# Low-rank weights and small constants prepared behind the first half's transposed input, and three low parts of the second half's input made by ScalarE and GpSimd

## The chip, the cores and the metric

The kernel runs on one core of one Trainium2 chip. The metric is the device time of one execution in microseconds; several runs are taken and their median is given. The engines are TensorE (PE: matmul, with PEld for its weight loads), VectorE (DVE), ScalarE (ACT), GpSimd (POOL) and SyncE (SP), which issues nearly all DMAs.

## The reference

One layer of a hybrid decoder trunk over a sequence of 1024 tokens with 1024 channels, in float32: a token mixer and a gated feed-forward part, each between two RMS norms.

```python
h = _rms_norm(x, norm_pre_mix)
# mixer: one projection p = h @ w_in; two groups of its columns
u, q = p[..., :1024], p[..., 1024:]
q = q + (_token_shift(q) - q) * mu            # r, k, v and the low-rank inputs wd, ad, gd
wf = decay_w0 + tanh(wd) @ decay_up           # decay of the recurrence
a  = sigmoid(iclr_a0 + ad @ iclr_up)
g  = sigmoid(gd) @ gate_up
y  = _wkv7(r, decay, k, v, -kk, kk * a)       # recurrence over the tokens, 8 heads of 64
rwkv_out = (_head_group_norm(y) + bonus) * g
c = silu(_layer_norm(_causal_dwconv(u[..., :512] * sigmoid(u[..., 512:]), cconv_w, 31 taps)))
x = x + _rms_norm(concat([rwkv_out, c]) @ w_out, norm_post_mix)
# feed-forward: ffn_up, a causal convolution of 3 taps, gelu(gate) * up, ffn_down
x = x + _rms_norm(_conv_ffn(_rms_norm(x, norm_pre_ffn)), norm_post_ffn)
```

## The kernel before

A float32 matmul is made of three faster ones: each operand is split into a high part (rounded to the matmul's type, float32r) and a low part (what the rounding left), and high times high, high times low and low times high are summed in one PSUM bank. A weight tile arrives as `wr`; ScalarE casts it to `wh` (L168), GpSimd subtracts to get `wl` (L168). The input of the projections is split in the same way, into the pairs `h`.

The 1024 tokens are worked in two halves of 512. For a half, `load_rows` (L307) loads four blocks of 128 token rows, `norm_rows` (L324 to L328) scales each row by its inverse norm, and `channels` (L280 to L295) transposes the rows by TensorE (L155) into PSUM banks and takes from each bank two readings: ScalarE writes the high part with the norm's gain as scale (L293), VectorE the low part (L295). A bank is free for TensorE again only when both have read it. There are two banks each with the tags `pe` and `pb`; `channels` takes them in the turn `pe`, `pb`, `pb`. In the first half a bank holds two channel tiles of 256 tokens, in the second half one tile of 512 tokens.

The first half's projections (`project`, into a `pb` bank) come right behind its transposes. The second half's transposes stand in the middle of the first half's work: VectorE then runs the 31 taps of the causal convolution (L432), each adding to one accumulator in the bank `pc`, and the first projections of the second half follow.

At the start `setup_mixer` also loads the two low-rank weights (`decay_up` and `iclr_up`, stacked in `lora`), casts them on ScalarE into `lw` (L254), subtracts their low rows on GpSimd (L256), and prepares small constants from the parameter table on VectorE (L260 to L269): one minus mu, halves of some biases, and halved convolution taps.

The order on each engine is made when the kernel is built: a scheduler takes the instructions by the priority of the stream in which they were written (`PRIO`; lower numbers come first, and parts under `high_priority` before others), with its own idea of how long each takes. `issue_after` holds the instructions written under it behind a given one. A change in one place can therefore also move instructions far behind it. One such stretch is the end of the mixer: there the last recurrence chunks, the convolution's layer norm (`conv_norm`: transposes `pc<-const,co`, norm, transposes `pc<-const,t`, then L453 on ScalarE, which writes `co`), the first nine feed-forward columns (`ffn_pair`: matmuls `pb<-f`, evacuation L911, a gelu L931), and the output projection (matmuls `pb<-wm,l`, its input split by L168 into `l<-mixr` and `l<-co`) share the engines. Each change between the functions of L453 and L931 costs ScalarE a table load.

DMAs are issued by SP in one queue; a new one waits until the one eight places before it has landed. The parameter table `params` holds the norm's gain, which L293 and L295 read.

Of the kernel before, what the change touches and what calls it, by code (L numbers as in the profile page):

```python
# [13 lines left out]
F32 = mybir.dt.float32  # L14
F32R = mybir.dt.float32r
BF16 = mybir.dt.bfloat16
AF = mybir.ActivationFunctionType
ALU = mybir.AluOpType
# [4 lines left out]
P = 128  # L23
# [3 lines left out]
HALF = 512  # L27
# [4 lines left out]
D_RWKV = 512  # L32
# [4 lines left out]
CONV_W = 31  # L37
# [32 lines left out]
POFF = {}  # L70
# [30 lines left out]
class Trunk:  # L101
# [130 lines left out]
    def setup_mixer(self, ctx):  # L232
        nc, tc, a = self.nc, self.tc, self.a
        pool = lambda name, bufs=1: ctx.enter_context(tc.tile_pool(name=name, bufs=bufs))
        cp = pool("mconst")
        self.mix = pool("mix")
        self.banks = {"pb": 2, "pc": 1, "pe": 2}
        self.xs = [self.psum.tile([P, 512], F32, name=f"xs{g}") for g in range(2)]
        self.wa = cp.tile([P, HALF], F32, name="wa")

        self.dw = cp.tile([P, 16 + 1024], F32, name="dw")
        nc.gpsimd.memset(self.dw[0:64, 528:1040], 0.0)
        self.Y = self.psum.tile([P, 512], F32, name="Y")


        self.lora = cp.tile([G_LORA, D_RWKV], F32, name="lora")
        nc.sync.dma_start(self.lora, a["lora"][:G_LORA, 2])
        self.lw = cp.tile([96, 2, D_RWKV], F32R, name="lw")  # L250
        for e in range(2):
            raw = self.wtile("wr", [P, D_RWKV])
            nc.sync.dma_start(raw, a["lora"][:, e])
            nc.scalar.copy(self.lw[:, e], raw[0:96])  # L254
            low = self.lw[64:96, e]
            nc.gpsimd.tensor_tensor(low, raw[64:96], low.bitcast(F32), ALU.subtract)  # L256
        self.lx = cp.tile([96, 2, QUARTER], F32R, name="lx")
        n = POFF["k_k"]
        self.omu = cp.tile([P, n], F32, name="omu")
        nc.vector.tensor_scalar(self.omu, self.params[:, :n], -1.0, 1.0, ALU.mult, ALU.add)  # L260

        self.hw0 = cp.tile([P, 8], F32, name="hw0")
        nc.vector.tensor_scalar(self.hw0, self.params[:, POFF["w0"]:POFF["w0"] + 8], 0.5, None, ALU.mult)
        self.ka = cp.tile([P, 8], F32, name="ka")
        ka = self.params[:, POFF["k_a"]:POFF["k_a"] + 4]
        nc.vector.tensor_scalar(self.ka[:, 0:4], ka, 0.5, None, ALU.mult)
        nc.vector.tensor_scalar(self.ka[:, 4:8], ka, -0.5, 1.0, ALU.mult, ALU.add)
        cw = self.params[:, POFF["cw"]:POFF["cw"] + 4 * CONV_W]
        nc.vector.tensor_scalar(cw, cw, 0.5, None, ALU.mult)  # L269
        self.carry = cp.tile([P, n], F32, name="carry")  # L270
        self.ccarry = cp.tile([P, 4, 32], F32, name="ccarry")[:, :, :CONV_W - 1]


    def channels(self, rows, gname, hs, toks, tags=("pn",), diags=None):


        nc = self.nc
        n = len(rows) * P
        per = 512 // n
        for b, k0 in enumerate(range(0, KT, per)):  # L280
            ps = self.bank(tags[b % len(tags)])
            for i in range(per):
                k = k0 + i
                for t, row in enumerate(rows):
                    o = (k % 4) * P
                    out, src = ps[:, i * n + t * P:i * n + (t + 1) * P], row[k // 4][:, o:o + P]
                    if diags is None:
                        self.transpose(out, src)
                    else:
                        self.mm(out, src, diags[t])  # L290
            parts = [(self.par(gname, k0 + i), ps[:, i * n:(i + 1) * n], *hs[k0 + i]) for i in range(per)]
            for g, pv, hi, lo in parts:
                self.mark_hi = nc.scalar.activation(hi[:, toks], pv, AF.Copy, scale=g)  # L293
            for g, pv, hi, lo in parts:
                self.mark_lo = nc.vector.scalar_tensor_tensor(lo[:, toks], pv, g, hi[:, toks].bitcast(F32), ALU.mult, ALU.subtract)  # L295

# [563 lines left out]
    def norm_ffn(self, h, row, piece, hs, ahead=2, tags=("pn",), dg=None, pool=None):  # L860
# [16 lines left out]
        for t in range(4):  # L877
            if t == ahead:
                channels(0)
            tt = 4 * h + t  # L880
            rs = slice(tt * P, (tt + 1) * P)
            x, s = row(), sf[:, t]
            nc.sync.dma_start(x, self.a["x"][rs])
            for c in range(2):
                m = piece()
                nc.sync.dma_start(m, self.mixd[rs, cut(c)])
                nc.vector.scalar_tensor_tensor(x[:, cut(c)], m, r[:, 4 + t:5 + t], x[:, cut(c)], ALU.mult, ALU.add)
                nc.scalar.activation(m, x[:, cut(c)], AF.Square, accum_out=s[:, c:c + 1])
            nc.sync.dma_start(self.x1d[rs], x)
            nc.vector.tensor_tensor(s[:, 2:3], s[:, 0:1], s[:, 1:2], ALU.add)  # L890
            self.rstd(s[:, 3:4], s[:, 2:3], 1.0 / D, RMS_EPS)
            if dg is None:
                nc.scalar.activation(x, x, AF.Copy, scale=s[:, 3:4])
            else:
                nc.vector.tensor_scalar(dg[:, t], self.con("ident"), s[:, 3:4], None, ALU.mult)
                diags.append(dg[:, t])
            rows.append((x[:, :512], x[:, 512:]))
            yield
        if ahead == 4:
            channels(0)  # L900
            yield
        channels(1)

    def taps(self, h, i, br, ps, acc):
# [371 lines left out]
    def mixer(self, sts):  # L1276
        nc, tc = self.nc, self.tc
# [78 lines left out]

        def channels(rows, hs):
            with self.stream("norm"):
                self.channels(rows, "pre_mix", hs, slice(0, HALF), ("pe", "pb", "pb"))

        cut = lambda t: (t[:, :512], t[:, 512:])
        with self.stream("norm"):
            two = [self.tl("l8", [P, 2, D]) for _ in range(2)]
            rows = [cut(two[t // 2][:, t % 2]) for t in range(4)]
            with self.stream("first"):
                self.load_rows(0, rows)
            hs = self.pairs("h")
            for b in range(2):
                two = rows[2 * b:2 * b + 2]
                self.norm_rows(two)  # L1370
                self.channels(two, "pre_mix", hs, slice(b * QUARTER, (b + 1) * QUARTER), ("pe", "pb", "pb"))
        self.R = self.tl("r", [P, NH, CH])
        nc.vector.memset(self.R[64:128], 0.0)
        project(0, hs, "k0 w k1 r0 r1")
        with self.stream("norm"):
            two = self.tl("mixr", [P, 2, D])
            rows = [cut(two[:, t]) for t in range(2)]
# [10 lines left out]
        project(0, hs, "u2 u3")  # L1388
        hs = self.pairs("h")
        channels(rows, hs)  # L1390
        mixes[0] = self.tl("mixr", [P, 4, HALF])
        prepare(1)
# [106 lines left out]
```

## Time and profile before

| | us |
|---|---|
| median of 3 runs | 1254.76 (1251.8 to 1254.91) |
| the profiled execution | 1252.95 |
| its span in the profile | 1251.2 |
| mean granted TensorE clock | 0.987 |
| busy: VectorE, ScalarE, GpSimd | 900.3, 729.4, 507.3 |

The profile gives for each engine what it ran and when, in us from the start of the span. A row of the timeline reads: start, duration, engine, line, operation, output<-input, how many were merged into the row, and, in brackets, how long the engine had been idle before it and what ended that. A row of the stage windows reads: the stretch and its length, then the busy time of TensorE, its weight loads, VectorE, ScalarE and GpSimd, each with its number of instructions, then the granted TensorE clock (1.00 is full), the DMA engines' busy share and GB/s.

### The profile page before, as it was taken

What the parts mean: (1) busy time and instruction counts of PE and PEld (TensorE: products, weight loads), DVE (VectorE), ACT (ScalarE), POOL (GpSimd) and SP (SyncE); (2) the same over time, 40 slices, a digit from 0 to 9 for tenths busy, and PEclk for the clock granted to TensorE, in tenths of its full rate; (3) what the DMA queues carried; (4) which work ended last, traced back from release to release, by engine and by line L of the source; (5) the groups of instructions that cost most, each with busy time, mean ns of one, the idle gap of its engine ahead of it and who ended that gap; (6) DMA issues with size and microseconds to landing.
All of it is one profiled execution on the core that took longest, in us unless ns stands there. A gap on an engine that the chain in (4) does not pass through costs nothing.

```text
span 1251.2 us, 22983 instructions
## 1 busy us (share of the span) xinstructions
PE 1204.7 (96%) x8424; PEld 985.3 (79%) x8424; DVE 900.3 (72%) x1558; ACT 729.4 (58%) x1515; POOL 507.3 (41%) x447
## 2 busy tenths in 40 slices
PE   5989998999999989999999999999999999999997
PEld 4767776787778977878889888888888888888886
DVE  5285998898669999998630655666656679479668
ACT  6563564565954676566752577876555566545452
POOL 4343330001103331354463499998888850000002
PEclk8999998999999999999999999999999999999999
DMA  7645442333343362222364798894222335337413
GB/s 244 177 122 141 134 135 64 97 123 125 110 125 93 99 200 96 77 86 77 110 181 120 287 314 299 294 310 151 85 75 77 101 128 169 99 109 223 133 59 134
DMA packets 102912, 180.97 MB, mean 145 GB/s; under 512 B 14896, under 2 KB 21424, under 8 KB 102800
## 3 DMA queue, kind: packets, MB, share of 16 engines
q1 hardware_dynamic: 102800, 179.51, 46.0%
q8 instruction: 66, 1.08, 0.4%
q14 instruction: 46, 0.38, 0.1%
HBM read 138.44 MB, written 41.03 MB: 143 GB/s over the span
## 4 chain that ended last, share of the span: by engine, by line
PE 62%; DVE 6%; DMA 1%; ACT 1%; issue 1%; POOL 0%; POOLq 0%; DVEq 0%; ACTq 0%
PE pb L140 27%; PE xs L140 16%; PE pe L140 14%; PE Y L140 2%; PE pc L140 2%; DVE pc L432 2%; DMA pt<-mixd 1%; PE pc L155 1%; DMA mixd<-t 0%; PE pe L155 0%; DVE m L168 0%; DVE sub L607 0%; DVE x L1123 0%; DVE dw L609 0%; DVE t L798 0%
## 5 line engine op out<-in xcount | busy, mean ns | idle before, releaser
L168 POOL TENSOR_TENSOR wl<-wr,wh 128x512 fp32r<-128x512 f32 (+1 forms) x175 | 230.0, 1316 | 218.2 <-ACT wh L168 183.9
L140 PE MATMUL pb<-h,wh 128*128 128x512 f32 (+3 forms) x720 | 229.0, 397 | 3.1 <-ACT wh L168 1.6
L140 PE MATMUL pb<-f,wh 128*128 128x512 f32 x648 | 203.7, 395 | 2.1 <-ACT wh L168 1.7
L168 ACT CAST wh<-wr 128x512 fp32r<-128x512 f32 (+1 forms) x214 | 131.4, 615 | 126.1 <-issue 37.3
L432 DVE SCALAR_TENSOR_TENSOR pc<-c,params,pc 128x512 f32<-128x512 f32 x232 | 174.3, 751 | 8.1 <-ACT pc L429 4.1
L140 PEld LDWEIGHTS pb<-h,wh 128*128 128x128 f32 (+2 forms) x720 | 131.5, 188 | 35.8 <-ACT wh L168 3.7
L140 PE MATMUL pb<-h,wl 128*128 128x512 f32 (+3 forms) x360 | 146.2, 406 | 2.2 <-POOL wl L168 2.0
L140 PEld LDWEIGHTS pb<-f,wh 128*128 128x128 f32 x648 | 121.1, 189 | 27.9 <-ACT wh L168 2.1
L140 PE MATMUL pb<-f,wl 128*128 128x512 f32 x324 | 128.7, 398 | 0.9 <-POOL wl L168 0.9
L162 POOL TENSOR_TENSOR ss<-var,mhalf 128x1 f32<-128x1 f32 x16 | 12.9, 810 | 221.0 <-DVE var L161 220.2
L1077 POOL TENSOR_TENSOR b<-b,b 128x512 f32<-128x512 f32 x72 | 93.2, 1297 | 2.1 <-DMA b<-ffn_down 0.7
L140 PEld LDWEIGHTS pb<-h,wl 128*128 128x128 f32 (+2 forms) x360 | 67.4, 187 | 20.7 <-POOL wl L168 4.6
L140 PE MATMUL xs<-f,wh 128*128 128x512 f32 x240 | 74.2, 390 | 0.4 <-DVE act L974 0.4
L168 POOL TENSOR_TENSOR wl<-b,wh 128x512 fp32r<-128x512 f32 x48 | 65.8, 1372 | 19.3 <-ACT wh L168 19.3
L140 PEld LDWEIGHTS pb<-f,wl 128*128 128x128 f32 x324 | 61.2, 189 | 14.8 <-POOL wl L168 2.2
L168 ACT CAST wh<-b 128x512 fp32r<-128x512 f32 x48 | 29.7, 618 | 59.9 <-PE pb L140 20.5
L140 PE MATMUL pe<-f,wh 128*128 128x512 f32 x208 | 64.1, 389 | 0.0
L722 POOL TENSOR_TENSOR XG<-r,GE 64x256 f32<-64x256 f32 x30 | 19.9, 666 | 87.5 <-DVE r L741 82.8
L140 PEld LDWEIGHTS xs<-f,wh 128*128 128x128 f32 x240 | 44.9, 188 | 10.1 <-DVE act L974 0.8
L193 ACT CAST wh<-wr 128x512 fp32r<-128x512 f32 (+2 forms) x44 | 26.5, 604 | 43.5 <-PE pb L140 31.1
L168 ACT CAST a<-act 128x512 fp32r<-128x512 f32 x50 | 30.0, 619 | 33.4 <-PE Y L140 18.9
L168 ACT CAST w<-wr 128x512 fp32r<-128x512 f32 x38 | 23.5, 622 | 40.9 <-PE Y L140 20.0
(421 smaller groups left out, 2948.8 us busy)
## 6 DMA issues: line engine op xcount, KB each, us to landing
wr<-ffn_up SPq DMA_DIRECT2D x99, 256.0 KB, 3.3
wr<-w_in SPq DMA_DIRECT2D x80, 256.0 KB, 2.9
b<-ffn_up SPq DMA_DIRECT2D x52, 256.0 KB, 2.7
b<-ffn_down SPq DMA_DIRECT2D x44, 256.0 KB, 4.6
sums<-b SPq DMA_DIRECT2D x44, 256.0 KB, 4.2
wr<-sums SPq DMA_DIRECT2D x44, 256.0 KB, 2.7
lows<-wl SPq DMA_DIRECT2D x40, 256.0 KB, 3.3
wl<-lows SPq DMA_DIRECT2D x40, 256.0 KB, 2.7
```

What stands on the lines that cost most here:

```text
L140: return self.nc.tensor.matmul(out, lhsT, rhs, start=start, stop=stop, skip_group_check=skip)
L155: self.nc.tensor.transpose(out, in_, self.con("ident")[:n, :n])
L162: self.nc.gpsimd.tensor_tensor(out, v[:, :n], self.mhalf[:, :n], ALU.pow)
L168: return self.nc.scalar.copy(hi, src), eng.tensor_tensor(lo, src, hi.bitcast(F32), ALU.subtract)
L193: self.nc.scalar.copy(hi, raw)
L432: nc.vector.scalar_tensor_tensor(out, c[:, j:j + HALF], w(j), acc, ALU.mult, ALU.add)
L722: nc.gpsimd.tensor_tensor(x[64:128], R[64:128, gs], w.GE[64:128, c, gs].unsqueeze(2).broadcast_to([64, 4, CH]), ALU.mult)
L1077: sub = lambda o, x, y, op=ALU.subtract: self.nc.gpsimd.tensor_tensor(o, x, y, op)
```

## The change

Three things change in the code. The low-rank weights and the small constants move from `setup_mixer` into a function of their own, `setup_later`, which is called behind the first half's transposed input: the weights are held behind its last high part, the constants behind its last low part. The low-rank weights are loaded into buffers with the tag `t2` instead of weight buffers. And in the second half, for the channel tiles 1, 3 and 5, VectorE no longer makes the low part: ScalarE copies the scaled tile in full precision into an SBUF buffer `pt`, and GpSimd subtracts the high part from it.

```diff
 def setup_mixer(self, ctx):
     self.lw = cp.tile([96, 2, D_RWKV], F32R, name="lw")
-    for e in range(2):
-        raw = self.wtile("wr", [P, D_RWKV])
-        nc.sync.dma_start(raw, a["lora"][:, e])
-        nc.scalar.copy(self.lw[:, e], raw[0:96])
-        low = self.lw[64:96, e]
-        nc.gpsimd.tensor_tensor(low, raw[64:96], low.bitcast(F32), ALU.subtract)
...
-    nc.vector.tensor_scalar(self.omu, self.params[:, :n], -1.0, 1.0, ALU.mult, ALU.add)
...
+def setup_later(self):
+    nc = self.nc
+    with self.tc.issue_after(self.mark_hi.ins):
+        for e in range(2):
+            raw = self.tl("t2", [P, D_RWKV])
+            nc.sync.dma_start(raw, self.a["lora"][:, e])
+            nc.scalar.copy(self.lw[:, e], raw[0:96])
+            low = self.lw[64:96, e]
+            nc.gpsimd.tensor_tensor(low, raw[64:96], low.bitcast(F32), ALU.subtract)
+    with self.tc.issue_after(self.mark_lo.ins):
+        nc.vector.tensor_scalar(self.omu, self.params[:, :POFF["k_k"]], -1.0, 1.0, ALU.mult, ALU.add)
...
 def channels(self, rows, gname, hs, toks, tags=("pn",), diags=None, pooled=()):
...
+    if k0 in pooled:
+        for g, pv, hi, lo in parts:
+            whole = self.tl("pt", [P, HALF])
+            nc.scalar.activation(whole, pv, AF.Copy, scale=g)
+            nc.gpsimd.tensor_tensor(lo[:, toks], whole, hi[:, toks].bitcast(F32), ALU.subtract)
+        continue
...
-    self.channels(rows, "pre_mix", hs, slice(0, HALF), ("pe", "pb", "pb"))
+    self.channels(rows, "pre_mix", hs, slice(0, HALF), ("pe", "pb", "pb"), pooled=(1, 3, 5))
...
         self.channels(two, "pre_mix", hs, slice(b * QUARTER, (b + 1) * QUARTER), ("pe", "pb", "pb"))
+    self.setup_later()
```

Line numbers of the changed kernel are about 10 higher behind the first edit (L293 is then L297, L453 is L463). The order of the instructions moves at three places.

First, SP's queue at the start of the program, from the last rows of the first half's input on (`l`, then `params`, `lora`, the weights `wr`, and `mixr`, the second half's rows). Before:

```order
L307 DMA l_4_129<-x 128x512 x4
L218 DMA params<-params 128x370
L219 DMA const<-consts 128x449
L249 DMA lora<-lora 96x512
L253 DMA wr_109<-lora 128x512
L253 DMA wr_113<-lora 128x512
L185 DMA wr_274<-w_in 128x512
```

And with the change:

```order
L317 DMA l_2_116<-x 128x512 x4
L185 DMA wr_274<-w_in 128x512
L185 DMA wr_281<-w_in 128x512
L185 DMA wr_340<-w_in 128x512
L218 DMA params<-params 128x370
L219 DMA const<-consts 128x449
L249 DMA lora<-lora 96x512
L265 DMA t_41_257<-lora 128x512
```

Three loads of projection weights now stand ahead of the parameters; on ScalarE two weight casts stand ahead of the first high part, and the low-rank casts behind the last one.

Second, VectorE at the second half's transposed input (`h`: low parts, `pc`: convolution taps). Before:

```order
L295 SCALAR_TENSOR_TENSOR h_1938<-pe_1953,params,h_1937 128x512
L432 SCALAR_TENSOR_TENSOR pc_1737<-c_1659,params,pc_1737 128x512
L295 SCALAR_TENSOR_TENSOR h_1940<-pb_1960,params,h_1939 128x512
L295 SCALAR_TENSOR_TENSOR h_1942<-pb_1967,params,h_1941 128x512
L432 SCALAR_TENSOR_TENSOR pc_1737<-c_1659,params,pc_1737 128x512
L295 SCALAR_TENSOR_TENSOR h_1944<-pe_1974,params,h_1943 128x512
L432 SCALAR_TENSOR_TENSOR pc_1737<-c_1659,params,pc_1737 128x512
L295 SCALAR_TENSOR_TENSOR h_1946<-pb_1981,params,h_1945 128x512
L295 SCALAR_TENSOR_TENSOR h_1948<-pb_1988,params,h_1947 128x512
```

And with the change:

```order
L305 SCALAR_TENSOR_TENSOR h_1938<-pe_1953,params,h_1937 128x512
L442 SCALAR_TENSOR_TENSOR pc_1737<-c_1659,params,pc_1737 128x512 x2
L305 SCALAR_TENSOR_TENSOR h_1942<-pb_1969,params,h_1941 128x512
L442 SCALAR_TENSOR_TENSOR pc_1737<-c_1659,params,pc_1737 128x512 x2
L305 SCALAR_TENSOR_TENSOR h_1946<-pb_1985,params,h_1945 128x512
```

The low parts of the tiles 1, 3 and 5 are gone, and two taps now stand between the others.

Third, ScalarE at the end of the mixer, up to the cast of the last feed-forward weight ahead of the output projection (`wh_7018` before, `wh_7024` with the change). Before:

```order
L168 CAST l_1098_7317<-mixr_5246 128x512 x4
L168 CAST wh_7000<-wr_6998 128x512
L453 ACT_TABLE_LOAD
L453 ACTIVATE co_4614<-pc_6245,params 128x128
L453 ACTIVATE co_4647<-pc_6245,params 128x128
L453 ACTIVATE co_6096<-pc_6245,params 128x128
L453 ACTIVATE co_6129<-pc_6245,params 128x128
L168 CAST wm_7343<-wr_7341 128x512
L168 CAST l_1100_7319<-co_4614 128x512
L168 CAST l_1100_7319<-co_4647 128x512
L168 CAST l_1100_7319<-co_6096 128x512
L168 CAST l_1100_7319<-co_6129 128x512
```

And with the change:

```order
L941 ACTIVATE pt_6910<-pt_6910 128x512
L168 CAST wh_6964<-wr_6962 128x512
L168 CAST l_1101_7323<-mixr_5252 128x512 x4
L168 CAST wh_6982<-wr_6980 128x512
L921 ACTIVATE pt_6952<-pb_6915,params 128x512
L923 COPY ecarry<-pb_6915 128x2
L168 CAST wh_7006<-wr_7004 128x512
L168 CAST wm_7349<-wr_7347 128x512
L168 CAST wh_7024<-wr_7022 128x512
L921 ACTIVATE pt_6998<-pb_6961,params 128x512
L923 COPY ecarry<-pb_6961 128x2
L463 ACT_TABLE_LOAD
```

Before, `wh_7018` follows directly on the rows shown, behind the four `l<-co`; with the change `wh_7024` stands ahead of the table load of L463. Ahead of the rows shown with the change stand, without any weight cast between them, an evacuation (L921) with its carry copy (L923), four gate activations (L781), a table load, four `co` activations (L463) and another table load (L941).

More of the change, by code (lines that the diff above doesn't have):

```diff
@@ L259, in setup_mixer, with channels @@
         self.omu = cp.tile([P, n], F32, name="omu")
-        nc.vector.tensor_scalar(self.omu, self.params[:, :n], -1.0, 1.0, ALU.mult, ALU.add)
         self.hw0 = cp.tile([P, 8], F32, name="hw0")
-        nc.vector.tensor_scalar(self.hw0, self.params[:, POFF["w0"]:POFF["w0"] + 8], 0.5, None, ALU.mult)
         self.ka = cp.tile([P, 8], F32, name="ka")
[L265 to L269, printed above, removed]
         self.carry = cp.tile([P, n], F32, name="carry")
         self.ccarry = cp.tile([P, 4, 32], F32, name="ccarry")[:, :, :CONV_W - 1]
-    def channels(self, rows, gname, hs, toks, tags=("pn",), diags=None):
+    def setup_later(self):
[9 more added lines that the diff above has]
+            nc.vector.tensor_scalar(self.omu, self.params[:, :POFF["k_k"]], -1.0, 1.0, ALU.mult, ALU.add)
+            nc.vector.tensor_scalar(self.hw0, self.params[:, POFF["w0"]:POFF["w0"] + 8], 0.5, None, ALU.mult)
+            ka = self.params[:, POFF["k_a"]:POFF["k_a"] + 4]
+            nc.vector.tensor_scalar(self.ka[:, 0:4], ka, 0.5, None, ALU.mult)
+            nc.vector.tensor_scalar(self.ka[:, 4:8], ka, -0.5, 1.0, ALU.mult, ALU.add)
+            cw = self.params[:, POFF["cw"]:POFF["cw"] + 4 * CONV_W]
+            nc.vector.tensor_scalar(cw, cw, 0.5, None, ALU.mult)
+    def channels(self, rows, gname, hs, toks, tags=("pn",), diags=None, pooled=()):
         nc = self.nc
```

## The prediction

> **What bounds the kernel.** I read the page first (busy shares, then the chain that ended last), then TensorE's waits, then the timeline and stage windows of the three places that the change touches.
>
> ```profile
> PE 1204.7 (96%) x8424; PEld 985.3 (79%) x8424; DVE 900.3 (72%) x1558; ACT 729.4 (58%) x1515; POOL 507.3 (41%) x447
> PE pb L140 <- ACT wh L168: 3.3, 3, 1.7
> 769.34 10.88 PE pb L140 x48
> ```
>
> TensorE is busy 1204.7 of 1251.2 us, so whatever another engine saves is worth only what it takes from the remaining 46.5 us, or from stretches where the clock was down. Its longest single wait for a weight's cast, 1.7, comes back in place three. From the chain's steady stretch, a 512-column matmul takes 10.88 / 48 = 0.227 us. That is the unit below.
>
> **Place one: the start.** Removed ahead of the first matmul: two casts of the low-rank weights on ScalarE, five small VectorE instructions, two GpSimd subtractions. Moved forward on SP's queue: three weight loads, now ahead of the parameters.
>
> ```profile
> 11.59 0.17 DVE L260 TENSOR_SCALAR omu<-params 128x14 f32<-128x14 f32 x1
> 11.90 0.84 ACT L293 ACTIVATE h<-pe,params 128x256 fp32r<-128x256 f32 x2 [0.99 <-PE pe L155]
> 12.63 0.72 ACT L327 ACTIVATE l<-l,ss 128x512 f32<-128x512 f32 x1
> 13.24 0.84 ACT L293 ACTIVATE h<-pb,params 128x256 fp32r<-128x256 f32 x2
> 13.60:17.00 3.40, 1.61 (x9) 0.96 (x8) 1.92 (x6) 3.40 (x9) 2.30 (x2) 1.00 1.05 387
> 15.09 0.61 ACT L254 CAST lw<-wr 96x512 fp32r<-96x512 f32 x1
> 18.27 1.58 ACT L293 ACTIVATE h<-pb,params 128x256 fp32r<-128x256 f32 x4
> 19.28 1.65 DVE L295 SCALAR_TENSOR_TENSOR h<-pb,params,h 128x256 fp32r<-128x256 f32 x4
> 20.30 0.77 PE L140 MATMUL pb<-h,wh 128*128 128x256 f32 x2 [0.48 <-DVE h L295]
> 23.83 0.58 PE L140 MATMUL pb<-h,wl 128*128 128x256 f32 x1 [0.21 <-POOL wl L168]
> 20.40:23.90 3.50, 3.29 (x15) 3.00 (x15) 3.50 (x8) 3.25 (x10) 1.28 (x1) 0.50 0.47 174
> ```
>
> The parameters were first read at 11.59; I take 11.4 for their landing. Three loads of 256 KB are 786 KB; at 387 GB/s (the window's last number) they take 2.0 us, so the parameters now land at about 13.4, and the first high part, which needs them for its scale, starts at about 13.5 instead of 11.90. In return ScalarE has less to do from there on. By start-to-start distances a pair of high parts costs about 0.75 (two pairs in 1.58), a row scaling 0.61 (12.63 to 13.24, 0.11 under its duration), a cast likewise about 0.5. Before: 8 pairs, two scalings, two low-rank casts and one weight cast, 6.0 + 1.2 + 1.5 = 8.7, from 11.90 to 20.6. Now: 8 pairs and one scaling, 6.6, from 13.5 to 20.1; the weight casts and the other scaling fall into the wait for the parameters. The first projection waits for the low part of the sixth pair (its bank) and the last transposes; 20.30 becomes about 20.0. The 0.21 wait for the second weight's low part goes too, since that weight is loaded 8 places earlier. TensorE runs at 0.50 of its clock here, so 0.3 us earlier is worth half: **0.15 + 0.2, about 0.3 us gained.** Parameters 1 us later than estimated would make it a loss of 0.5; parameters on time as before would gain 1.0: bounds +0.5 to -1.0. The moved instructions then stand between the last high part and the second half's norms, which TensorE reads only in place two; VectorE's five cost about 0.1 each there. If that cover were gone they would cost 1.2 on ScalarE.
>
> **Place two: the second half's transposed input.** Three of eight low parts leave VectorE; ScalarE makes three full-precision copies, GpSimd three subtractions.
>
> ```profile
> 187.81 0.69 ACT L293 ACTIVATE h<-pe,params 128x512 fp32r<-128x512 f32 x1
> 188.40 1.26 ACT L293 ACTIVATE h<-pb,params 128x512 fp32r<-128x512 f32 x2
> 189.32 0.75 DVE L295 SCALAR_TENSOR_TENSOR h<-pe,params,h 128x512 fp32r<-128x512 f32 x1
> 190.12 0.44 PE L155 MATMUL pe<-const,mixr 128*128 128x128 f32 x2 [1.62 <-DVE h L295]
> 190.63 1.40 DVE L295 SCALAR_TENSOR_TENSOR h<-pb,params,h 128x512 fp32r<-128x512 f32 x2
> 191.44 0.44 PE L155 MATMUL pb<-const,mixr 128*128 128x128 f32 x2 [0.66 <-DVE h L295]
> 194.73 0.69 PE L155 MATMUL pb<-const,mixr 128*128 128x128 f32 x2 [0.52 <-DVE h L295]
> 195.49 1.20 PE L140 MATMUL pb<-h,wh 128*128 128x512 f32 x2
> 197.88 4.71 DVE L432 SCALAR_TENSOR_TENSOR pc<-c,params,pc 128x512 f32<-128x512 f32 x6
> 188.30:191.70 3.40, 1.12 (x8) 0.69 (x7) 3.36 (x6) 1.94 (x4) 0.00 (x0) 1.00 0.00 0
> 195.10:198.50 3.40, 3.40 (x11) 2.82 (x10) 3.40 (x6) 1.17 (x2) 0.00 (x0) 0.50 0.00 0
> 160.67 1.28 POOL L168 TENSOR_TENSOR wl<-wr,wh 128x512 fp32r<-128x512 f32 x1 [2.21 <-ACT wh L168]
> 160.79 1.72 DVE L525 TENSOR_TENSOR pt<-pt,row 128x512 f32<-128x512 f32 x1
> 183.30 0.68 DVE L525 TENSOR_TENSOR pt<-pt,row 128x512 f32<-128x512 f32 x1
> L432 DVE SCALAR_TENSOR_TENSOR pc<-c,params,pc x114: 724/756/757, 135.0 to 299.9; 128x512 f32<-128x512 f32 x114
> ```
>
> Each transposed tile's bank must be read by both parts before TensorE reuses it. VectorE holds the banks, since conv taps stand between its low parts. The reorder fills the freed places with taps: two taps now separate the remaining low parts. Two taps of one accumulator cost 0.78 each (4.71 / 6), a tap beside a low part 0.66. Counting on from the first low part at 189.32: taps at 189.98 and 190.77, low part of tile 2 at 191.43 (before: 191.29), two taps, tile 4 at 193.54 (before 193.92). So the first wait (1.62) stays, the 0.66 goes because ScalarE's copy frees tile 1's bank at 189.7, tile 5's transposes come 0.15 later, tile 7's 0.38 earlier, and the first projection starts at 195.11 instead of 195.49. Tile 5's own bank, released by ScalarE at about 194.5, isn't last. At half clock that is about 0.2 to 0.38: **about 0.3 us**, bounds 0 and 1.5. ScalarE, busy 1.94 of 3.40 in the first window, has room for 3 x 0.6; GpSimd idles, and its results (191.0, 192.7, about 195.8 at 1.28 each) are needed later. The cover gone, a late GpSimd part would cost its 1.28. VectorE's saving of 3 x 0.66 sits beside a full TensorE and pays nothing more.
>
> GpSimd can slow VectorE: the subtraction of two SBUF tiles at L525 took 1.72 beside a GpSimd subtraction, 0.68 alone. Taps and low parts read one operand from PSUM; the 114 taps lie within 724 to 757 ns, whatever GpSimd did, so I price this at zero. The Trainium skill, SBUF, "Who interferes with whom", has the same condition: a VectorE instruction with two SBUF inputs contends with a GpSimd one that reads SBUF. The Trainium skill, Perfetto Trace Analysis, "Optimizing Scalar/DVE Operations", puts it wider, that offloading between these two might not help because they share a read port; by that, three blockings of 1.28 would make this place 3.8 minus 2.0 slower.
>
> **Place three: the end of the mixer.** Nothing in the diff touches it, but the order there is made anew, and it holds a stall.
>
> ```profile
> 616.48 0.60 PE L155 MATMUL pe<-const,mixr 128*128 128x128 f32 x4
> 616.92 1.06 PE L140 MATMUL pe<-gd,lora 96*128 96x128 f32 x8
> 618.98 1.49 ACT L771 ACTIVATE mixr<-pe,params 128x128 f32<-128x128 f32 x4
> 624.89 1.28 ACT L453 ACT_TABLE_LOAD   x1
> 626.19 1.51 ACT L453 ACTIVATE co<-pc,params 128x128 f32<-128x128 f32 x4
> 628.08 2.19 ACT L168 CAST l<-co 128x512 fp32r<-128x512 f32 x4
> 630.17 0.63 ACT L168 CAST wh<-wr 128x512 fp32r<-128x512 f32 x1
> 628.76 0.39 PE L140 MATMUL pb<-f,wl 128*128 128x512 f32 x1
> 630.85 0.73 PE L140 MATMUL pb<-f,wh 128*128 128x512 f32 x2 [1.70 <-ACT wh L168]
> ```
>
> The last weight's cast stands on ScalarE behind a table load, four activations and five casts. TensorE ends at 629.15, waits 1.70, then another 0.93 for GpSimd's low part, and the clock falls: its last 12 matmuls run from 630.85 to 636.32, 5.47 instead of 2.72.
>
> ```profile
> 632.51 0.79 PE L140 MATMUL pb<-f,wl 128*128 128x512 f32 x1 [0.93 <-POOL wl L168]
> 636.32 11.66 PE L140 MATMUL pb<-wm,l 128*128 128x256 f32 x96
> ```
>
> Lost: 1.70 + 2.75 = **4.45 us**. In the new order that cast stands ahead of the table load and the l<-co casts, so it goes. What is late next? The weight cast two places before it (wh_6964): ahead of it now stand an evacuation, four gate activations, a table load, four co activations, another load and a gelu: 0.7 (as a 0.69 high part) + 1.4 + 1.3 + 1.4 + 1.3 + 0.5 = 6.6, then the cast, 0.5. TensorE starts that batch with its last matmul before the gate; until it wants the weight it has 24 matmuls (5.4), 12 transposes (0.44 for four, 616.48 to 616.92) and 8 gate matmuls (0.7): 7.4. The cast is just in time, GpSimd's part (1.28) is not: about 0.9 late. The projection's weights, behind l<-co, another load and a gelu, I put 0.6 late. **Net 4.45 - 1.5, about 3.0 us**; bounds: all of it (4.45), or the same stall elsewhere (0).
>
> **Sum.** 0.3 + 0.3 + 3.0 = 3.6 us. The profiled execution took 1252.95 (span 1251.2), so 1249.4. The median shown is 1254.76, with runs from 1251.8: 1.8 above the execution that the sum starts from, so a median may lie as much higher.
>
> **Rivals.** *The stall moves, 1252.3.* If the two table loads ahead of wh_6964 wait for VectorE's taps and it comes 2 us later, TensorE idles about 3 there, loses clock as before, and only places one and two remain. For: ScalarE had no gap from 624.89 to 630.80. Against: those taps need only the evacuation that starts the batch. *The same cast 4 us late, 1255.5*: idle 4.9, clock 1.8, the projection's 0.6, against 4.45 + 0.6: 2 to 3 slower; it decides from about 2.5 us of lateness. *The clock holds, 1246.5.* It fell after a window with 1.12 of 3.40 busy; tile 4's transposes now join that window. At full clock the 3.0 us up to 198.50 shrink by 1.5, and a tail without any new stall adds 1.5. The Trainium skill, TensorE: Matmul & The Clock Gate, "What's actually happening", asks for a whole idle window of about 3.4 us before the clock falls; this trace shows it fall with a third of one busy, so I give the rival little. *The change does not do what it says*: parameters later than 15 us would turn place one into a loss of 1 to 2.
>
> **How the numbers follow.** Forecast 0.45, clock holds 0.15, stall moves or place one fails 0.28, slower 0.12. About 0.3% (3.8 us) is what a measurement of this kernel can tell from no change; the forecast lies at that edge, so a little over half of it counts as faster: 0.43. Slower by that much needs the third rival at its worst: 0.11; within: 0.46. The range, 1244.5 to 1256, takes in all four cases and leaves out the ends.
>
> **What would show it.** First high part at 13.5 and first projection at 20.0; second half's first projection 0.4 earlier after its transposes; no ScalarE wait in the last 24 matmuls before the output projection, but one of about 1 us for GpSimd some 50 matmuls earlier. Wrong: a first projection after 21, or TensorE's idle time between 500 and 640 above 3 us.

## The result and the profile after

| | before | with the change |
|---|---|---|
| median, us (8 runs each) | 1252.24 (1251.48 to 1254.91) | 1258.49 (1257.11 to 1264.78) |
| the profiled execution, its span | 1252.95, 1251.2 | 1258.65, 1256.9 |
| granted TensorE clock | 0.987 | 0.988 |

The changed kernel takes 1.0051 times the time of before (95% interval 1.0038 to 1.0064): 6.2 us slower by the medians, where 1249.4 was forecast and the range ended at 1256.

The page of the changed kernel, its line of busy times:

```profile
PE 1205.4 (96%) x8424; PEld 984.4 (78%) x8424; DVE 902.6 (72%) x1555; ACT 731.4 (58%) x1518; POOL 510.7 (41%) x450
```

TensorE does the same work in the same busy time (before 1204.7). The span grew by 5.7, and what TensorE does not fill grew from 46.5 to 51.5: the loss is waiting. TensorE's waits in the changed kernel (what it waited for, us in all, how often, longest):

```profile
PE pb L140 <- POOL wl L168: 3.9, 6, 1.1
PE pb L140 <- ACT wh L168: 3.2, 4, 1.4
PE pe L155 <- ACT h L297: 2.9, 1, 2.9
PE pb L140 <- DVE kk L905: 2.3, 1, 2.3
PE pb L140 <- DVE f L305: 2.2, 3, 1.1
PE pc L155 <- DVE t L458: 1.3, 1, 1.3
```

The 1.70 for the last weight's cast is gone, as forecast; the longest wait for a cast is now 1.38, at another place, and the waits of 2.3 and 1.3 for VectorE's `kk` and `t` are new. Where the time went shows when the same work is compared in both traces, here by the start of a few TensorE instructions:

| the same work | before | after | later by |
|---|---|---|---|
| third group of transposes at the start | 10.96 | 11.22 | 0.26 |
| first projection | 20.30 | 21.10 | 0.80 |
| 61st matmul `pb<-h,wh` | 38.67 | 42.35 | 3.68 |
| first transposes of the second half | 177.12 | 180.75 | 3.63 |
| first projection behind them | 195.49 | 198.73 | 3.24 |
| end of the 1.58 wait for `dw` | 458.82 | 462.29 | 3.47 |
| 11th matmul `xs<-wm,l` of the output projection | 649.02 | 655.10 | 6.08 |
| end of the span | 1251.2 | 1256.9 | 5.7 |

So 3.4 were lost between 11 and 42 us, 0.4 won at the second half's transposes, and 2.6 lost in the last 190 us of the mixer.

**The start.** First before, VectorE and ScalarE, then the same work with the change, both from the timeline:

```profile
11.74 0.16 DVE L266 TENSOR_SCALAR ka<-params 128x4 f32<-128x4 f32 x1
12.39 0.48 DVE L328 TENSOR_SCALAR l<-l,ss 128x512 f32<-128x512 f32 x1
25.03 1.34 ACT L327 ACTIVATE mixr<-mixr,ss 128x512 f32<-128x512 f32 x2 [1.38 <-POOL ss L162]
26.97 0.62 ACT L168 CAST wh<-wr 128x512 fp32r<-128x512 f32 x1 [0.60 <-PE pb L140]
```

```profile
12.56 1.27 POOL L168 TENSOR_TENSOR wl<-wr,wh 128x512 fp32r<-128x512 f32 x1
12.63 1.48 DVE L338 TENSOR_SCALAR l<-l,ss 128x512 f32<-128x512 f32 x1
13.95 0.84 ACT L297 ACTIVATE h<-pe,params 128x256 fp32r<-128x256 f32 x2 [0.51 <-DMA params<-params]
14.49 1.26 POOL L168 TENSOR_TENSOR wl<-wr,wh 128x512 fp32r<-128x512 f32 x1
14.56 1.48 DVE L338 TENSOR_SCALAR l<-l,ss 128x512 f32<-128x512 f32 x1 [0.44 <-POOL ss L162]
...
22.12 2.54 POOL L268 TENSOR_TENSOR lw<-t,lw 32x512 fp32r<-32x512 f32 x2 [6.37 <-ACT lw L266]
22.43 1.01 DVE L270 TENSOR_SCALAR omu<-params 128x14 f32<-128x14 f32 x1
23.43 1.26 DVE L273 TENSOR_SCALAR ka<-params 128x4 f32<-128x4 f32 x1
24.80 1.27 DVE L327 BATCH_NORM_STATS2 bs<-mixr 128x6 f32<-128x512 f32 x2
28.20 1.33 ACT L337 ACTIVATE mixr<-mixr,ss 128x512 f32<-128x512 f32 x2 [3.23 <-POOL ss L162]
29.44 0.60 ACT L168 CAST wh<-wr 128x512 fp32r<-128x512 f32 x1
30.09 0.73 PE L140 MATMUL pb<-h,wh 128*128 128x512 f32 x2 [1.38 <-ACT wh L168]
31.47 0.65 PE L140 MATMUL pb<-h,wl 128*128 128x512 f32 x1 [0.64 <-POOL wl L168]
```

Two things are to be seen. A row scaling of VectorE (`l<-l,ss`) that took 0.48 now takes 1.48, twice, and both times it starts 0.07 behind a GpSimd subtraction `wl` and ends 0.3 behind its end: the weights loaded ahead of the parameters brought these subtractions there. And the small constants stand beside the two low-rank subtractions: 0.17 and 0.16 became 1.01 and 1.26, and the second of these ends with GpSimd, at 24.7. Behind them queue VectorE's statistics of the second half's rows (24.80, before 21.63), then GpSimd's inverse norm, then ScalarE's scaling of those rows (28.20, before 25.03), and behind that the cast of a weight that TensorE wants at once. It waits 1.38 and 0.64, and the clock falls. The stage windows of the changed kernel, then of before:

```profile
28.10:31.50 3.40, 1.38 (x9) 0.74 (x7) 2.84 (x6) 3.30 (x6) 3.21 (x5) 1.00 0.00 0
31.50:34.90 3.40, 3.40 (x8) 2.64 (x9) 1.02 (x3) 1.38 (x3) 1.28 (x1) 0.52 0.53 155
```

```profile
31.50:34.90 3.40, 3.35 (x15) 2.33 (x13) 0.00 (x0) 1.12 (x4) 0.74 (x1) 1.00 0.56 164
```

At 0.52 instead of 1.00 another 1.6 of 3.4 is lost; with the waits 3.6, of which the vanished 0.21 and the later start of the half-clock matmuls take a part back: between the first projection and the 61st `pb<-h,wh` 2.9 are lost.

**The second half's transposes.** TensorE's waits there in the changed kernel, from the timeline:

```profile
193.75 0.69 PE L155 MATMUL pe<-const,mixr 128*128 128x128 f32 x2 [1.62 <-DVE h L305]
197.96 0.69 PE L155 MATMUL pb<-const,mixr 128*128 128x128 f32 x2 [0.27 <-DVE h L305]
```

The 1.62 stays, the 0.66 is gone, and the way from the first transposes to the projection is 17.98 instead of 18.37. Half clock, however, lasts 10.2 us there (192.1 to 202.3) instead of 6.8 (191.8 to 198.7) and ends 3.60 behind the projection instead of 3.16. That takes 0.2 of the 0.4 back, and by the wait for `dw` the changed kernel is late by 3.47 again.

**The end of the mixer.** Stage windows of the changed kernel, and of before shifted by about the same work:

```profile
500.00:550.00 50.00, 48.77 (x654) 38.41 (x653) 47.93 (x80) 28.20 (x57) 17.15 (x15) 1.00 0.24 70
550.00:600.00 50.00, 49.50 (x386) 39.57 (x386) 42.68 (x70) 28.45 (x65) 23.80 (x20) 1.00 0.28 80
600.00:641.00 41.00, 38.76 (x217) 30.11 (x216) 24.06 (x40) 27.61 (x54) 18.87 (x16) 1.00 0.35 110
```

```profile
496.50:546.50 50.00, 50.00 (x633) 39.80 (x632) 47.45 (x80) 28.12 (x56) 17.25 (x15) 1.00 0.25 76
546.50:596.50 50.00, 49.90 (x424) 40.35 (x421) 44.66 (x71) 29.02 (x66) 25.36 (x21) 1.00 0.29 80
596.50:637.50 41.00, 38.37 (x218) 30.94 (x217) 26.61 (x42) 31.70 (x60) 21.16 (x17) 0.96 0.40 120
```

TensorE's idle time in the three stretches is now 1.23, 0.50 and 2.24 (before 0.00, 0.10, 2.63): the stall at 630 and its half clock are gone, but waits took their place. The ones that stand out in the last 190 us, from the timeline of the changed kernel:

```profile
476.11 0.75 DVE L897 SCALAR_TENSOR_TENSOR row<-pt,nr,row 128x512 f32<-128x512 f32 x1 [2.23 <-DMA pt<-mixd]
477.11 0.71 PE L140 MATMUL pb<-kk,row 128*128 128x128 f32 x4 [2.34 <-DVE kk L905]
502.89 0.70 PE L140 MATMUL pb<-f,wh 128*128 128x512 f32 x2 [1.10 <-DVE f L305]
635.87 0.63 PE L155 MATMUL pc<-const,t 128*128 128x128 f32 x4 [1.28 <-DVE t L458]
```

### The profile page after: what moved, and what is told of

It reads as the page before. It is cut to its first block, busy times and chain, and to the rows that moved or that the text cites. A ratio compares the mean times of both kernels' runs of the same rounds, so it can differ in the third digit from the quotient of the medians.

```text
span 1256.9 us, 22980 instructions
## 1 busy us (share of the span) xinstructions
PE 1205.4 (96%) x8424; PEld 984.4 (78%) x8424; DVE 902.6 (72%) x1555; ACT 731.4 (58%) x1518; POOL 510.7 (41%) x450
## 4 chain that ended last, share of the span: by engine, by line
PE 60%; DVE 6%; issue 2%; ACT 2%; DMA 1%; POOL 1%; POOLq 0%; DVEq 0%; ACTq 0%
PE pb L140 25%; PE xs L140 16%; PE pe L140 14%; DVE pc L442 2%; PE Y L140 2%; PE pc L140 2%; POOL wl L168 1%; PE pc L155 1%; DMA wr<-w_out 0%; DVE dw L619 0%; DMA pt<-mixd 0%; DVE pt L930 0%; DVE l L631 0%; DMA wr<-ffn_up 0%; PE pe L155 0%
```

## The experiments

My theory from the two traces: the start costs about 4 because of GpSimd work beside VectorE's small instructions, and the remade order at the end of the mixer costs the rest. The rivals: that the moved instructions cost by their mere place in the queues, whatever GpSimd does; and that everything behind the start is chance of the clock. To compare executions whose starts differ by up to 0.7 us for the same code, the table gives three stretches of each profiled execution: **A** from the third group of transposes at the start to the first projection, **B** from there to the 61st `pb<-h,wh`, **C** from the end of the wait for `dw` to the 11th `xs<-wm,l`. The ratios are to before in the same series, whose median was 1252.34, 1252.66 and 1252.54 in the three series (`setup_only` to `s_both`, `tail` to `r_wlp_pf_tail`, and the last three kernels), from 12 runs of most kernels (`s_lows` 5, `s_both` 6, `lows_behind` 11); A, B and C come from one trace of each kernel; C is left out where the order on the way there is another one altogether.

| kernel | median | ratio (95%) | A | B | C |
|---|---|---|---|---|---|
| before (profiled) | | | 9.34 | 18.37 | 190.2 |
| the change (profiled) | 1258.49 | 1.0051 (1.0038 to 1.0064) | 9.88 | 21.25 | 192.8 |
| setup_only | 1256.57 | 1.0028 (1.0019 to 1.0037) | 9.90 | 21.05 | 189.9 |
| pooled_only | 1255.23 | 1.0019 (1.0008 to 1.0029) | 9.48 | 17.89 | 193.0 |
| s_lows | 1265.44 | 1.0097 (1.0081 to 1.0114) | 10.56 | 19.04 | |
| s_both | 1265.36 | 1.0087 (1.0067 to 1.0107) | 8.73 | 17.42 | |
| tail | 1252.18 | 0.9990 (0.9974 to 1.0006) | 9.34 | 18.01 | 191.1 |
| p2 | 1253.65 | 1.0004 (0.9990 to 1.0018) | 9.34 | 18.14 | 191.4 |
| q_ab | 1257.82 | 1.0037 (1.0021 to 1.0053) | 10.29 | 21.77 | 189.5 |
| r_wlp_pf_tail | 1256.41 | 1.0020 (1.0005 to 1.0035) | 8.77 | 21.60 | 191.0 |
| lows_behind | 1253.52 | 1.0007 (0.9996 to 1.0018) | 9.87 | 17.97 | 189.6 |
| after_lows_behind | 1256.92 | 1.0027 (1.0016 to 1.0037) | 10.23 | 17.67 | 192.5 |
| start_all | 1256.86 | 1.0021 (1.0009 to 1.0033) | 9.30 | 18.53 | 192.4 |

**The two halves of the change.** `setup_only` is the changed kernel without its third part; its order behind the start is that of before. `pooled_only` is before with the third part alone; its order from the second half's transposes on is that of the change.

```diff
  setup_only, against the changed kernel
-    self.channels(rows, "pre_mix", hs, slice(0, HALF), ("pe", "pb", "pb"), pooled=(1, 3, 5))
+    self.channels(rows, "pre_mix", hs, slice(0, HALF), ("pe", "pb", "pb"))
  pooled_only, against before
-    self.channels(rows, "pre_mix", hs, slice(0, HALF), ("pe", "pb", "pb"))
+    self.channels(rows, "pre_mix", hs, slice(0, HALF), ("pe", "pb", "pb"), pooled=(1, 3, 5))
```

> The start of the change without the pooled low parts; from the second projections on every engine has the order of before. Theory A (the terms are local: the start costs 3.4 us, the new order at the end of the mixer 3.0, and it belongs to the pooled part): 3 to 4 us slower than before, about 1255.7 against 1252.2; TensorE waits 1.4 and 0.6 for the fourth weight's two parts near 30 us as in the changed kernel, and the stretch from 467 to 641 us of before takes 173.4 us, as before. Theory B (a late start shifts everything behind it, and the stretch at the end of the mixer is slow because of that): 6 us slower, about 1258, with some 3 us more in that stretch.

> The pooled low parts without the change at the start; from there on every engine has the order of the changed kernel. Theory A: 2 to 3 us slower than before, about 1254.8: 0.5 gained at the second half's transposed input, 3.0 lost between 467 and 641 us. Theory B: no slower than before, 1251.5 to 1252.5.

Measured: +4.2 and +2.9 us, together 7.1 against 6.2 for both, so the halves add up within their intervals, close to theory A (3 to 4 and 2 to 3). The timeline of `setup_only` has the start's trouble (and its two row scalings take 1.49 and 1.48):

```profile
24.07 1.27 DVE L273 TENSOR_SCALAR ka<-params 128x4 f32<-128x4 f32 x1
32.13 0.80 PE L140 MATMUL pb<-h,wl 128*128 128x512 f32 x1 [0.65 <-POOL wl L168]
```

and keeps C at 189.9. `pooled_only` keeps A and B, gains at the second half's transposes, and loses 2.8 in C, the wait for the late load `pt<-mixd` among it; its timeline:

```profile
472.66 0.71 PE L140 MATMUL pb<-kk,row 128*128 128x128 f32 x4 [2.58 <-DVE kk L901]
```

**Is it GpSimd's overlap or the mere place?** `s_lows` is `setup_only` with only the two low-rank subtractions held back, behind a one-column GpSimd instruction that reads the second half's last scaled row; the constants stay where the change has them. `s_both` holds the first two weight subtractions as well, behind the first half's last row scaling.

```diff
  s_lows, against setup_only
-                low = self.lw[64:96, e]
-                nc.gpsimd.tensor_tensor(low, raw[64:96], low.bitcast(F32), ALU.subtract)
+                self.raws.append(raw)
...
+    def setup_last(self):
+        with self.tc.issue_after(self.guard().ins):
+            for e, raw in enumerate(self.raws):
+                low = self.lw[64:96, e]
+                self.nc.gpsimd.tensor_tensor(low, raw[64:96], low.bitcast(F32), ALU.subtract)
  s_both, against s_lows, around the split of each weight
+                    if self.gate is not None and self.made < 2:
+                        gate.enter_context(self.tc.issue_after(self.gate.ins))
...
```

> As setup_only, but GpSimd's two low-rank subtractions stand behind the second half's last row scaling (a one-column GpSimd instruction that reads it holds them there). Theory C (GpSimd's subtractions hold VectorE's small constants for 2 us, so the second half's norm comes late, and ScalarE's scaling of its rows stands ahead of the fourth weight's cast): the constants take 0.15 to 0.2 each instead of 1.0 and 1.3, the first scaling of the second half's rows starts at about 26.2 instead of 28.2, the cast that was waited for at 30.1 is done by 28.5, and TensorE's waits of 1.4 and 0.6 go: the projections at 36 us stand 0.5 to 1.5 behind before instead of 3.9. Theory D (the two low-rank casts on ScalarE and the later first half make the norm late): the scaling starts at 27.5 or later and a wait of 1 us or more stays near 30 us. The scheduler makes the order behind the start anew, so the total can stand up to 3 us on either side of what the start gives.

> As s_lows, and GpSimd's first two weight subtractions are held behind the first half's last row scaling in the same way. Theory C: VectorE's scalings of the first half's third and fourth row blocks take 0.5 instead of 1.5, the low parts follow 1 us earlier, and the first projection starts at 20.0 to 20.3 instead of 21.1. Theory E (the late parameters, read at 13.95, set the start): the first projection stays at 20.8 to 21.1. The total again within 3 us of what the start gives.

Measured: the constants fell to 0.17 to 0.22 in the same place in the queue, the row scalings in `s_both` to 0.49, A to 8.73 and B to 17.42, both shorter than before. The timeline of `s_both`:

```profile
13.64 0.49 DVE L354 TENSOR_SCALAR l<-l,ss 128x512 f32<-128x512 f32 x1 [0.44 <-POOL ss L163]
14.35 2.50 POOL L169 TENSOR_TENSOR wl<-wr,wh 128x512 fp32r<-128x512 f32 x2
20.06 0.47 PE L141 MATMUL pb<-h,wh 128*128 128x256 f32 x2 [0.47 <-DVE h L320]
```

So the start loses by the overlap, not by the place. As whole kernels both are misses: the scheduler made the order far behind anew, and 10 to 13 us were lost between 180 and 500, which says nothing of the start.

**Is the last batch's stall worth 4.45, and where does C's loss come from?** `tail` is before with the four casts `l<-co` held behind the cast of the last feed-forward weight, which moves ScalarE's order there; VectorE's moves by one place, TensorE's and GpSimd's not at all. `p2` pools one tile only, which gives TensorE, VectorE, ScalarE and GpSimd the change's order from 217 us on, without most of the rest. `q_ab` tries another cover for the low-rank subtractions (behind the fourth inverse norm of the second half, with the constants not held), and `r_wlp_pf_tail` adds to it the parameters loaded first, the first two weight subtractions behind the first half's last inverse norm, and `tail`.

```diff
  tail, against before
+                if h and k == 4:
+                    gate.enter_context(self.tc.issue_after(last.ins))   # last: cast of the last feed-forward weight
  p2, against before, with the changed channels()
+                self.channels(rows, "pre_mix", hs, slice(0, HALF), ("pe", "pb", "pb"), pooled=(2,))
  q_ab, against s_lows
-        with self.tc.issue_after(self.mark_lo.ins):     # the constants
+        if True:
...
-        with self.tc.issue_after(self.guard().ins):
+        with self.tc.issue_after(self.pow.ins):
  r_wlp_pf_tail, against q_ab (besides the gate of s_both, here behind self.pow, and tail)
-        nc.sync.dma_start(self.params, a["params"])
+        with self.tc.high_priority():
+            nc.sync.dma_start(self.params, a["params"])
```

> The kernel before, with one thing moved: the output projection's four splits of the convolution's output stand on ScalarE behind the cast of the last feed-forward weight instead of ahead of it. Nothing else moves by more than two places. Theory A (the stall ahead of the output projection costs what the prediction gave it, 1.70 of waiting and 2.75 of half clock): neither wait of 1.7 or 0.9 is left there, the clock stays at 1.00, and the time falls by 3.0 to 4.5 us, to 1247.8 to 1249.3. Theory F (the wait moves to the output projection, which then waits for the splits): under 1 us gained, with a wait of over 2 us at the first matmuls of the output projection.

> The kernel before, with one low part of the second half's input (tile 2) made by ScalarE and GpSimd. TensorE's order stays that of before up to the middle of the kernel and is from there on that of the changed kernel. Theory A (the order alone costs 3 us at the end of the mixer): 2.5 to 3.5 us slower than before, 1255 to 1256, with waits of 2.3 to 2.6 us for VectorE near 477 us and of 1.3 us near 635 us. Theory G (the waits there come from what the three pooled parts do to the time of the second half): at most 1 us slower, without these waits.

> As setup_only (order of before from the projections on), but GpSimd's low-rank subtractions stand behind its last power of the second half's norm, and VectorE's constants are not held back. Theory C (contention at the constants makes the second half's norm and with it the fourth weight late): each constant takes 0.15 to 0.3 us, the second half's first row scaling starts at 26.0 to 26.8 instead of 28.2, and of setup_only's 4.2 us 2 to 3.5 come back: 1253 to 1254.5. Theory D (the low-rank casts and the late first half are the reason): within 1 us of setup_only, 1255.5 to 1257.5.

> q_ab with the parameters loaded ahead of the weights, GpSimd's first two weight subtractions behind its fourth power, and the moved splits of tail; TensorE's order is that of before but for some 30 places late. If the terms add (contention at the row scalings 1.0 us at half clock, late parameters 0.5, the tail 3 to 4.5): first projection at 19.5 to 20.2, and 1246.5 to 1249.5. If the low-rank subtractions, which now stand ahead of the third weight's, are what comes late there, TensorE waits 1 to 2 us for GpSimd near 29 us and the time is 1249 to 1251. Theory F: no faster than q_ab.

Measured: `tail` gains nothing that can be told (0.9974 to 1.0006). Its timeline shows the stall one engine further on:

```profile
630.05 0.64 ACT L168 CAST wh<-wr 128x512 fp32r<-128x512 f32 x1
630.25 1.29 POOL L168 TENSOR_TENSOR wm<-wr,wm 128x512 fp32r<-128x512 f32 x1 [1.76 <-ACT wm L168]
631.50 1.72 POOL L168 TENSOR_TENSOR wl<-wr,wh 128x512 fp32r<-128x512 f32 x1
633.27 0.51 PE L140 MATMUL pb<-f,wl 128*128 128x512 f32 x1 [1.70 <-POOL wl L168]
636.88 4.31 PE L140 MATMUL pb<-wm,l 128*128 128x256 f32 x34 [1.04 <-DVE pt L923]
```

The cast is early, but GpSimd takes a subtraction of the output projection first, as it does in before (there at 628.28), and TensorE waits the same 1.70 for `wl`, then 1.04 for VectorE. So the 4.45 was not to be had by moving the cast alone. `p2` shares the change's new waits in C (1.10 at 495.74, 1.28 at 628.72), but not the late load, and its C is 191.4. The traces with before's order and without the late load (before, `setup_only`, `q_ab`, `lows_behind`) have 189.5 to 190.2, so the new order costs 1.2 to 1.9 there; as a whole kernel `p2` is 1.0 slower, which can't be told from no change. `q_ab` and `r_wlp_pf_tail` are misses (by the medians 5.2 and 3.8 slower than before). They free the constants, yet B stays at 21.6 to 21.8: the low-rank subtractions now stand on GpSimd ahead of a weight's subtraction that TensorE waits for, as the timeline of `q_ab` has it:

```profile
28.18 2.69 POOL L286 TENSOR_TENSOR lw<-t,lw 32x512 fp32r<-32x512 f32 x2
30.95 2.50 POOL L168 TENSOR_TENSOR wl<-wr,wh 128x512 fp32r<-128x512 f32 x2
32.27 0.50 PE L140 MATMUL pb<-h,wl 128*128 128x512 f32 x1 [2.40 <-POOL wl L168]
```

**The cover that holds.** `lows_behind` is `setup_only` with the low-rank subtractions behind the sixth weight's subtraction, its order otherwise that of before; `after_lows_behind` is the whole change with the same edit; `start_all` is `lows_behind` with the parameters first and the first two weight subtractions behind the first half's last inverse norm.

```diff
  lows_behind and after_lows_behind, in setup_last as above
+        with self.tc.issue_after(self.made[5].ins):     # the sixth weight's subtraction
  start_all, against lows_behind
+                    if len(self.made) < 2:
+                        gate.enter_context(self.tc.issue_after(self.gate.ins))
...
+        with self.tc.high_priority():
+            nc.sync.dma_start(self.params, a["params"])
```

> As setup_only, but GpSimd's two low-rank subtractions stand behind its sixth weight subtraction instead of ahead of the third; TensorE, and every engine from the projections on, keep the order of before. Theory C: the constants take 0.2 us each, the second half's first row scaling starts at 25.8 to 26.3, the waits of 1.4 and 0.6 at 30 us go and no 2.4 us wait for GpSimd comes in their place; the projections near 38 us stand 0.8 to 1.6 behind before instead of 3.7 to 4.1, and of setup_only's loss of 4.2 us 2 to 3.5 come back: 1253 to 1254.5. Theory D: 1255.5 to 1257.5.

> The changed kernel with the same one thing moved; TensorE keeps the order of the changed kernel. Theory C: 2 to 3.5 us faster than the changed kernel, 1255 to 1256.5; what is left over before is the reordered end of the mixer and the row scalings at the start. Theory D: 1257.5 to 1259.

> As lows_behind, with the parameters loaded ahead of the weights and GpSimd's first two weight subtractions behind its fourth power, so that they stand beside at most one of the first half's row scalings. The order behind the start is made anew. Theory C: first projection at 19.5 to 20.3, and the projections near 38 us 1 to 3 us ahead of before: the start of the change would then have been a gain. Theory E (the parameters or something else set the start): first projection at 20.6 or later, the projections near 38 us level with before or behind it. The total depends on the new order by up to 12 us, as in s_both: 1249 to 1264.

Measured: `lows_behind` gets 3 of the 4.2 back and is level with before. Its timeline:

```profile
23.06 0.17 DVE L278 TENSOR_SCALAR ka<-params 128x4 f32<-128x4 f32 x1
26.74 1.34 ACT L348 ACTIVATE mixr<-mixr,ss 128x512 f32<-128x512 f32 x2 [1.28 <-POOL ss L163]
27.98 0.60 ACT L169 CAST wh<-wr 128x512 fp32r<-128x512 f32 x1
30.02 0.50 PE L141 MATMUL pb<-h,wl 128*128 128x512 f32 x1 [0.27 <-POOL wl L169]
```

B is 17.97 there and 17.67 in `after_lows_behind`, whose ratio falls from 1.0051 to 1.0027 (by the medians 6.2 become 4.4, a little less than expected); what it still loses lies in C (192.5) and A. In both the row scalings stay at 1.46 to 1.48 and A near 10. `start_all` freed one of the two (the other is still 1.49, beside a `wl` that starts 0.07 ahead of it): A is 9.30, but the order behind was made anew and cost more than that (C 192.4). No kernel here beats before by what can be told.

## Why the prediction was wrong

**Place one, 0.3 gained; lost 3.4 in the traces, 4.2 by `setup_only`.** Two steps failed. The first is "so I price this at zero": the price of GpSimd beside VectorE was asked only for taps and low parts, with the one row at hand (1.72 beside GpSimd, 0.68 alone) that has two SBUF inputs. The row scalings and the constants, which have one, were not asked, though the order showed weight loads moved ahead. By stretch A, the two held row scalings cost 1.2 to 1.8 (8.73 in `s_both` against 9.88 with the change and 10.56 in `s_lows`, its nearest neighbour in code). The sum itself was good: with the parameters at 13.95 (13.4 to 13.5 estimated) A would be 0.6 shorter than before, had they run free. The Trainium skill, SBUF — State Buffer, "Who interferes with whom", says more than I used: besides two-input instructions it names copy, cast and tensor_scalar, which can take the shared ports in their two-port modes, and whoever issues first keeps them for the whole instruction. The trace agrees: 0.48 became 1.48, beside a 1.27 subtraction that began 0.07 earlier, and taps and low parts, which read PSUM, kept their 0.72 to 0.76.

The second is "the moved instructions then stand between the last high part and the second half's norms, which TensorE reads only in place two". The norms have such a late reader, but the engine that applies them has another instruction behind them: ScalarE's queue holds the scaling of those rows ahead of a weight cast that TensorE wants at 28.7. The lost-cover price, 1.2, was too low as well, since it counted ScalarE's two casts, not VectorE's constants held for 2.3 by GpSimd, nor the clock. `lows_behind` shows it: with the overlap gone, B is back.

**Place two, 0.3 gained: right.** The 0.66 went, the 1.62 stayed, GpSimd's three subtractions cost nothing; 0.39 measured up to the first projection, of which the longer half clock took 0.2. The rival that the clock holds did not come: TensorE was busy 2.56 of the 3.40 us ahead (188.70 to 192.10), more than the 1.12 of before, and the clock fell all the same.

**Place three, 3.0 gained; lost 2.6.** The stall went, as said, and the lateness that the prediction counted in came at about its price: for the weight two places before, TensorE waited 0.23 for the cast and 0.62 for GpSimd (0.9 estimated), for the projection's weight 0.76 (0.6 estimated). Two steps failed.

"So it goes" put the whole 4.45 on the cast; `tail` shows that GpSimd's order decides the same batch, and that with the cast early TensorE waits 1.70 for `wl`. Nor did the half clock in the 4.45 belong to the stall: `setup_only` has the same two waits there (1.71 at 635.80, 0.92 at 637.45) and a granted clock of 1.00 from 634 to 644.

And "net 4.45 - 1.5" looked for new lateness along the casts of those last batches alone, while the order had been made anew for 190 us. At 635.87 TensorE now also waits 1.28 for `t`: VectorE takes its four low parts `l<-mixr` (4.25 us from 627.45) ahead of the layer norm's statistics (631.63), which came first in before (616.98, the low parts at 622.82). Another 1.10 is waited at 502.89. `p2` puts the new order at 1.2 to 1.9, and the rest of the 2.6 to 2.8 goes with the wait of 2.3 to 2.6 at `kk`: C is 192.5 to 193.0 in the three traces that have the order of the change and this wait, 191.4 in `p2`, which has the same order without it. The prediction's own signs of being wrong both came: a first projection after 21 (21.10), and more than 3 us idle between 500 and 640 (1.23 + 0.50 + 2.24 is 4.0; before 2.7).

The wait at `kk` comes from a load `pt<-mixd` that landed 5.40 us after its issue, 3.54 before. The order alone does not bring it: it appears with the order of the change (also in `pooled_only`, 5.63, and `after_lows_behind`, 5.51) and with before's order there (`tail`, 5.70, and `r_wlp_pf_tail`, 5.53), and `p2`, with the order of the change, has 3.80. A 16 KB packet of the instruction queue begins near the end of each of these loads, but 3.62 us after the issue in `tail`, where the load is long, and 3.14 in `p2`, where it is short, so it does not tell them apart. What holds the load stays open, and with one trace of each kernel also how often it happens.

The rival that ends slower, "the same cast 4 us late" (the prediction calls it the third where it works out its chances; it stands second), had the right sign for place three and the wrong instruction. Place one, where most of the loss is, was given a loss of 1 to 2 at worst, and only from late parameters.

## What to carry to other kernels

Before moving GpSimd work, list every VectorE instruction that will then stand beside it, the tiny ones too, and price each at GpSimd's whole duration unless a row of the trace shows that form unharmed. When instructions are hidden behind "what is read much later", follow each engine's queue, not only the data: the late reader's engine may hold something urgent behind it. And where an edit lets a scheduler remake a long stretch, one stall that goes is no gain until the other engines of the same batch and the rest of the stretch have been walked.

## What the runs showed of the hardware

A VectorE instruction of four elements per partition took 1.26 us instead of 0.16 beside a GpSimd subtraction: its size does not matter, only how long GpSimd still runs. GpSimd seems to be held in turn: its one-column inverse norm took 0.73 beside a row scaling, 0.55 ahead of it. And how busy TensorE was in a window of 3.40 us does not tell by itself whether the clock falls: it fell after 1.12 (188.30 to 191.70 of before), after 1.38 (28.10 to 31.50 of the changed kernel) and also after 2.56 (188.70 to 192.10 of the changed kernel), but not after 1.69 in `setup_only` (632.40 to 635.80).
